# A hybrid diffusion backbone on one core: four weight-staging slots, another slot spacing, and a reordered opening

## The chip, the cores and the metric

The kernel runs on one core of a Trainium2 chip. The metric is the device time of one execution, in microseconds; the median of several executions of the same program is what is compared. The core has a matrix engine (PE, with weight loads shown apart as PEld), a vector engine (DVE), a scalar engine (ACT), a general engine (POOL) and a sync engine (SP) that only issues transfers. On-chip memory has 128 partitions; all addresses below are bytes inside one partition.

## What is computed

Two layers over 1024 latent tokens and 256 context tokens of width 1024, all in float32. The reference, cut to its frame:

```python
for i in range(DEPTH):                      # DEPTH = 2
    sh1, sc1, g1, sh2, sc2, g2 = ada_mod(c, ada_w[i], ada_b[i])
    u_lat = modulate(rms_norm(h_lat, norm1_g[i]), sh1, sc1)
    # the same for the context stream, with c_ctx
    if even:                                # layer 0
        y_lat = mixer_ab(u_lat, *ab)        # Fourier channels || Hyena long convolutions
        y_ctx = mixer_ab(u_ctx, *ab)
    else:                                   # layer 1
        y_lat, y_ctx = mixer_na(u_lat, u_ctx, ...)   # 2-D neighbourhood attention
    h_lat = h_lat + g1 * y_lat
    h_lat = h_lat + g2 * swiglu(modulate(rms_norm(h_lat, norm2_g[i]), sh2, sc2), gate, up, down)
return rms_norm(h_lat, final_g)
```

`ada_mod` is `silu(cond) @ w + b`. The Hyena filters come from a small sine network on positions (`sin(freq * (z @ w1 + b1))`, twice, then `@ w3`), are windowed, summed and Fourier-transformed before they are multiplied with the spectrum of the input.

## The kernel before

**Precision.** A float32 product is made of three faster ones. An operand x is split into a rounded part `hi` (ACT, L323) and the rest `lo` (DVE, L325); then hi·hi, hi·lo and lo·hi are added up in PSUM. In the profile these products are the MATMULs of 512, 384 or 256 columns at L319, L1503, L1674 and L1786. Every MATMUL has a weight load (LDWEIGHTS) of its own. A few products, those of the opening's adaLN and sine network among them, are plain float32 and take two passes of PE each.

**Stages, in order of time.** Opening (0 to about 190 us): sine network (`filter_mlp`), raw filters (`filter_raw`, DVE at L665), adaLN vectors of layer 0 (`ada_first`), norms of the input (`norms`), and the spectrum of the filters in two halves (`filter_spectrum`, 32 matrices `ff_l` of 512 KB, loaded by `cast`). Then input projection, Fourier and Hyena mixing (to about 700), output projection and the context part of FFN 0 (to about 1000), the Winograd-like FFN 0 (`wino_steps`, L1503, then `down`, L1674), the values and attention (about 1640 to 2260), and FFN 1 to the end at 2974.

**Memory.** Tiles are taken from pools; a pool gives each tag a ring of slots. From low addresses up: the descriptor area of the GpSimd-issued transfers (16 KB), constants (`cp`, with a pad of PAD_C words), `p4` (S4 tiles, 20 of 4 KB), `p2` (S2 tiles, 35 of 2 KB), `pg` (G), `pt` (T, six of 2 KB, with a pad of PAD_T words), `pk` (TK) and `pw`, the weight pool. `pw` has three tags with two slots each: `wl`, `wh` and `ws`. `weights` (L343) loads a matrix block into `ws` and splits it into `wh` and `wl`; `cast` (L389) loads a float32r matrix straight into one of the three tags in turn; `mat` takes `wh` and `wl` in turn; `cmat` and `cmat2` load f16 into `ws` and copy into `wh`/`wl`. `shifted` (L330) takes a tile of 1056 words and starts at word 16 of it, which sets the slot's size: 1056 words, 4224 bytes.

Added up from the pools of the built program, the first S4 slot starts at 20672 (80 x 256 + 192) and every S4, S2, G and T slot a multiple of 2048 behind it. The weight pool starts at 203968 (796 x 256 + 192), and its slots are 4224 (16 x 256 + 128) apart. So modulo 256 the moving operands start at 192, and the two slots of each weight tag at 192 and at 64.

**What sets the order.** The program is written as generators that `run` steps by hand (`next(ada1)`, `next(fr)`, `next(ng)`), and a scheduler of the tile layer then orders each engine's instructions within what the buffers and dependences allow. SP issues most loads (`ld`, L304), POOL those of `ldr` (L310), each in order; a transfer waits on its queue for the completion counter that it shares with the eighth one before it.

**The opening as written** (`run`, from L2057). `setup` loads `mask` and `gs`, `ada_begin` loads `ada_b`; then come the four loads of the sine network, `cond`, two blocks of `w3`, ten `x_row` blocks of 512 KB (`norms`, first step), then both layers of the sine network (`drain(mlp)`), eight adaLN steps, the eight steps of `filter_raw` with an adaLN step each, and the spectrum.

Of the kernel before, what the change touches and what calls it, by code (L numbers as in the profile page):

```python
# [10 lines left out]
F32 = mybir.dt.float32  # L11
F32R = mybir.dt.float32r
F16 = mybir.dt.float16
# [5 lines left out]
P = 128  # L19
# [9 lines left out]
WID = {0: 512, 1: 512, 2: 256, 3: 256, 4: 256}  # L29
OFF = {0: 0, 1: 512, 3: 512, 4: 768}  # L30
KSTART = (0, 8, 24, 32)
PAD_C, PAD_T, SHIFT = 72, 112, 16
BOPS = ("B11", "B21", "T2", "T1", "T3", "B22", "T4")


# [201 lines left out]
class Builder:  # L237
    def __init__(self, ctx, tc, a, out, taps=None, stop=None):
        self.tc, self.nc, self.a, self.out = tc, tc.nc, a, out
        self.taps, self.stop = taps, stop  # L240
        ent = ctx.enter_context
        self.cp = ent(tc.tile_pool(name="cp", bufs=1))
        self.p4 = ent(tc.tile_pool(name="p4", bufs=20))
        self.p2 = ent(tc.tile_pool(name="p2", bufs=35))
        self.pg = ent(tc.tile_pool(name="pg", bufs=4))
        self.pt = ent(tc.tile_pool(name="pt", bufs=6))
        self.pko = ent(tc.tile_pool(name="pk", bufs=4))
        self.pw = ent(tc.tile_pool(name="pw", bufs=2))
# [45 lines left out]
    def PQ(self):  # L294
        return self.pq.tile([P, 512], F32, tag="pq", name=self.nm("pq"))

    def C(self, w, dt=F32, p=P):
        return self.cp.tile([p, w], dt, name=self.nm("c"), tag=self.nm("ct"))

# [25 lines left out]
        self.last_lo = eng.tensor_tensor(lo, src, hi.bitcast(F32), SUB).ins  # L325

    def pair2(self, tags=("wh", "wl")):
        return [self.pw.tile([P, 1024], F32R, tag=g, name=self.nm(n)) for g, n in zip(tags, ("wh", "wl"))]

    def shifted(self, tag, name, w=1024):  # L330

        return self.pw.tile([P, 1056], F32R, tag=tag, name=self.nm(name))[:, SHIFT:SHIFT + w]

    def pair1(self):
        return self.shifted("wh", "wh"), self.shifted("wl", "wl")

    def pair3(self):

        self.p3 = (getattr(self, "p3", 0) + 1) % 3
        tags = ("ws", "ws") if self.p3 == 0 else ("wh", "wl")  # L340
        return [self.shifted(g, n) for g, n in zip(tags, ("wh", "wl"))]

    def weights(self, src, w=1024, cut=False, keep=None, wide=False, load=None):  # L343
        st = self.S4() if wide else self.pw.tile([P, 1024], F32, tag="ws", name=self.nm("ws"))
        if keep:
            hi, lo = keep
        else:
            hi, lo = self.pair3() if wide == 3 else self.pair1() if wide == 2 else self.pair2()
        (load or self.ld)(st.rearrange("p (n k) -> p n k", n=4) if cut else st[:, :w], src)
        self.split(st[:, :w], hi[:, :w], lo[:, :w])  # L350
        return hi, lo

    def mat(self, w, dt=F32R):
        self.mk ^= 1
        return self.pw.tile([P, w], dt, tag=("wh", "wl")[self.mk], name=self.nm("mat"))

    def cmat(self, w, src, view=None, small=False, shift=False):

        if small:
            st, m = self.S2(F16), self.S2(F32R, w)  # L360
            self.ld(view(st[:, :w]) if view else st[:, :w], src)
            self.nc.scalar.copy(m, st[:, :w])
            return m
        st = self.pw.tile([P, w], F16, tag="ws", name=self.nm("cs"))
# [6 lines left out]
        self.nc.scalar.copy(m, st)  # L371
        return m

    def cmat2(self, src, shift=False):

        st = self.pw.tile([P, 2048], F16, tag="ws", name=self.nm("cs"))
# [12 lines left out]
    def cast(self, w, src):  # L389

        self.mj = (self.mj + 1) % 3
        m = self.pw.tile([P, w], F32R, tag=("wh", "wl", "ws")[self.mj], name=self.nm("mat"))
        self.ldr(m, src)
        return m

# [33 lines left out]
    def setup(self):  # L429
        nc, a = self.nc, self.a  # L430
        self.ident = self.C(P)
        make_identity(nc, self.ident)
        self.ones = self.C(P)
        nc.vector.memset(self.ones, 1.0)
        self.eps = self.C(1)
        nc.vector.memset(self.eps, EPS)
        self.mask = self.C(4)
        self.ld(self.mask, a["mask"])
        self.gs = self.C(40)
        self.ld(self.gs, a["gs"])  # L440


    def ada_begin(self):
        nc, a = self.nc, self.a
        self.ada = {(l, c): self.C(48) for l in (0, 1) for c in (0, 1)}
        self.adab = self.C(96)
        self.ld(self.adab, a["ada_b"])

    def ada_first(self):
# [134 lines left out]
    def filter_mlp(self):  # L584
# [12 lines left out]
        for layer, w in enumerate((w1, w2)):  # L597
# [11 lines left out]
            self.clamp = nc.vector.tensor_scalar(s, s, 3.1415925, -3.1415925, op0=MIN, op1=MAX).ins  # L609
            self.sin = nc.scalar.activation(s, s, AF.Sin).ins  # L610
# [840 lines left out]
    def wino_weights(self, src, done=None, half=None):  # L1451


        nc = self.nc
        st = []
        if half is not None:
            for x in src:
                for c in (0, 512):
                    st.append(half())
                    self.ld(st[-1], x[:, c:c + 512])  # L1460
            a11, a12, a21, a22 = st
        else:
            for x in src:
                st.append(self.pw.tile([P, 1024], F32, tag="ws", name=self.nm("ws")))
                self.ld(st[-1], x)
            a11, a12, a21, a22 = (t[:, c:c + 512] for t in st for c in (0, 512))
        w = {} if done is None else done
        if done is None:
            wh = self.pw.tile([P, 1024], F32R, tag="wh", name=self.nm("wh"))
            wl = self.pw.tile([P, 1024], F32R, tag="wl", name=self.nm("wl"))  # L1470
# [182 lines left out]
    def down(self, l, bops, sops, hidc, hs, h, todo, after, keep):  # L1653
# [5 lines left out]
        def operands(asrc, bsrc, own):  # L1659
            hi, lo = self.S4(F32R), self.S4(F32R)  # L1660
            f = lo.bitcast(F32)
            if own:
                f = self.S4() if own == 1 else self.pw.tile([P, 1024], F32, tag="ws", name=self.nm("ws"))
# [98 lines left out]
        if l == 0:  # L1762
# [4 lines left out]
            for kb in range(NFB):  # L1767
# [289 lines left out]
    def run(self):  # L2057
        nc, a = self.nc, self.a
        self.setup()
        self.ada_begin()  # L2060
        raws = {sq: ({}, {}) for sq in ("l", "c")}

        def weave(main, *others):
# [5 lines left out]
        def drain(g):  # L2069
            for _ in g:  # L2070
                pass
# [3 lines left out]
        def norms():  # L2075
# [72 lines left out]
        weave(self.filter_spectrum("l", 1, raws["l"][1]), (ng, 1))  # L2148
        drain(ng)
        self.load_cond()  # L2150
# [305 lines left out]
```

## Time and profile before

| | |
|---|---|
| median of 3 executions | 2973.5 us (2970.81 to 2974.62) |
| the profiled execution | 2975.74 us |
| its span, first to last instruction | 2974.0 us |
| mean granted TensorE clock over the span | 0.982 |
| PE busy | 2843.4 us (96%) in 15704 matmuls |
| weight loads busy | 2357.7 us (79%) |
| DVE, ACT, POOL busy | 2095.6 (70%), 1327.3 (45%), 530.2 (18%) us |
| transfers | 567.36 MB, mean 191 GB/s |

A row of the profile names the source line, the engine, the operation and the tiles as `out<-in`, with buffer numbers left out: `ps<-s,wh` is a product into PSUM with moving operand `s` (an S4 or S2 tile) and weights `wh`. A matmul's own duration includes its way through the array, so in a dense run the distance from one start to the next is the pace, and it is much smaller than the duration. In a table by stretches, the columns are the stretch, its length, busy time and count for each engine, the granted clock (PEclk), the share of the DMA engines and GB/s. Line numbers are those of the kernel before; in the changed kernel they are 3 to 6 higher.

### The profile page before, as it was taken

How to read it: one execution, taken by the hardware profiler on the slowest of the kernel's cores; microseconds unless marked ns; L12 is line 12 of the kernel's file. 1: busy time of each engine (PE TensorE's matmuls, PEld its weight loads, DVE VectorE, ACT ScalarE, POOL GpSimd, SP SyncE). 2: the span in 40 equal slices, each digit the busy share in tenths (PEclk: the TensorE clock that was granted, in tenths of full speed). 3: DMA queues.
4: the chain of work that ended last, by engine and by line, in shares of the span. 5: the costliest groups of instructions: out<-in, count | busy, mean ns of one | idle time of the engine just before them, and what ended most of it. 6: DMA issues, size and time to landing. Idle time of an engine off the chain costs nothing. (4 is left out here: it accounts for less than half of the span.)

```text
span 2974.0 us, 44537 instructions
## 1 busy us (share of the span) xinstructions
PE 2843.4 (96%) x15704; PEld 2357.7 (79%) x15704; DVE 2095.6 (70%) x3984; ACT 1327.3 (45%) x2496; POOL 530.2 (18%) x816
## 2 busy tenths in 40 slices
PE   8999999699999999999999999999999999999997
PEld 3778888487899787788888888788787788888886
DVE  5877796775677777777777537888777977755455
ACT  4443215353454333333445326777765533333442
POOL 2112023251101111212010002232222022112000
PEclk9999999899999999999999999999999999999998
DMA  7765455274555554658885435777856266435653
GB/s 279 265 231 174 165 167 176 76 255 151 211 172 193 177 178 171 212 195 307 317 293 166 134 128 137 175 185 183 226 178 217 103 233 216 163 107 198 205 192 120
DMA packets 304813, 567.36 MB, mean 191 GB/s; under 512 B 83528, under 2 KB 130314, under 8 KB 304590
## 3 DMA queue, kind: packets, MB, share of 16 engines
q1 hardware_dynamic: 245950, 380.45, 40.3%
q0 software_dynamic: 56336, 179.87, 17.4%
q10 hardware_dynamic: 2304, 4.20, 0.4%
q8 instruction: 123, 2.02, 0.3%
q14 instruction: 100, 0.82, 0.1%
HBM read 414.44 MB, written 119.80 MB: 180 GB/s over the span
## 5 line engine op out<-in xcount | busy, mean ns | idle before, releaser
L1503 PE MATMUL ps<-s,s 128*128 128x512 f32 x1992 | 497.4, 390 | 6.9 <-ACT tk L1508 2.9
L1503 PEld LDWEIGHTS ps<-s,s 128*128 128x128 f32 x1992 | 373.2, 188 | 89.9 <-ACT g L1508 4.2
L319 PE MATMUL ps<-s,wh 128*128 128x256 f32 (+1 forms) x1768 | 394.3, 329 | 1.1 <-ACT wh L323 1.1
L319 PEld LDWEIGHTS ps<-s,wh 128*128 128x128 f32 x1768 | 294.5, 190 | 37.1 <-ACT wh L323 3.2
L319 PE MATMUL pq<-s,wh 128*128 128x512 f32 (+1 forms) x984 | 301.5, 384 | 4.1 <-DVE s L1900 3.7
L323 ACT CAST wh<-ws 128x1024 fp32r<-128x1024 f32 (+1 forms) x139 | 142.3, 1025 | 346.5 <-PE ps L319 179.0
L325 DVE TENSOR_TENSOR wl<-ws,wh 128x1024 fp32r<-128x1024 f32 (+1 forms) x139 | 165.6, 1193 | 140.0 <-ACT wh L323 139.6
L1674 PE MATMUL ps<-s,s 128*128 128x512 f32 (+1 forms) x1000 | 258.4, 383 | 3.9 <-DVE s L325 3.8
L319 PE MATMUL ps<-s,wl 128*128 128x256 f32 (+1 forms) x884 | 255.8, 327 | 1.5 <-DVE wl L325 1.5
L323 ACT CAST s<-s 128x1024 fp32r<-128x1024 f32 (+2 forms) x184 | 168.3, 940 | 188.4 <-DMA s<-d 167.3
L319 PE MATMUL ps<-s,s 128*128 128x64 f16 (+4 forms) x2659 | 218.0, 235 | 15.9 <-DVE st L1972 8.4
L323 ACT CAST s<-t 128x512 fp32r<-128x512 f32 (+1 forms) x241 | 136.8, 590 | 202.9 <-DVE t L1482 87.8
L325 DVE TENSOR_TENSOR s<-s,s 128x1024 fp32r<-128x1024 f32 (+2 forms) x162 | 185.1, 1174 | 47.7 <-ACT s L323 47.3
L1674 PEld LDWEIGHTS ps<-s,s 128*128 128x128 f32 x1000 | 184.4, 188 | 42.3 <-DVE s L325 5.9
L319 PE MATMUL ps<-s,mat 128*128 128x512 f32 x756 | 196.1, 411 | 19.9 <-ACT s L323 16.8
L319 PEld LDWEIGHTS pq<-s,wh 128*128 128x128 f32 x984 | 179.6, 191 | 39.1 <-DVE s L1900 5.3
L325 DVE TENSOR_TENSOR s<-t,s 128x512 fp32r<-128x512 f32 (+1 forms) x241 | 167.6, 710 | 45.5 <-ACT s L323 20.2
L1503 PE MATMUL ps<-s,wh 128*128 128x512 f32 x608 | 193.4, 395 | 0.2 <-DVE g L1596 0.2
L319 PEld LDWEIGHTS ps<-s,mat 128*128 128x128 f32 x756 | 146.6, 197 | 58.1 <-ACT s L323 14.6
L319 PE MATMUL pq<-s,wl 128*128 128x512 f32 (+1 forms) x492 | 183.4, 382 | 0.0
L319 PEld LDWEIGHTS ps<-s,wl 128*128 128x128 f32 x884 | 163.2, 189 | 18.8 <-DVE wl L325 2.3
L1674 PE MATMUL ps<-s 128*128 128x512 f32 (+1 forms) x500 | 149.4, 385 | 0.0
(431 smaller groups left out, 5499.2 us busy)
## 6 DMA issues: line engine op xcount, KB each, us to landing
s<-d SPq DMA_DIRECT2D x282, 256.0 KB, 3.7
s<-in_down SPq DMA_DIRECT2D x150, 256.0 KB, 4.1
d<-s POOLq DMA_DIRECT2D x137, 256.0 KB, 3.6
d<-tk POOLq DMA_DIRECT2D x98, 256.0 KB, 3.4
s<-in_ada_w POOLq DMA_DIRECT2D x48, 512.0 KB, 4.9
g<-in_bias SPq DMA_DIRECT2D x128, 192.0 KB, 3.0
ws<-in_up SPq DMA_DIRECT2D x44, 512.0 KB, 3.7
d<-g POOLq DMA_DIRECT2D x87, 256.0 KB, 3.2
```

The lines of the kernel that those rows point to most:

```text
L319: self.nc.tensor.matmul(o, l, r, start=st, stop=sp)
L323: self.last_hi = nc.scalar.copy(hi, src).ins
L325: self.last_lo = eng.tensor_tensor(lo, src, hi.bitcast(F32), SUB).ins
L1503: nc.tensor.matmul(ps, x[:, sl], y, start=first and j == 0 and x is wh and y is xh, stop=j == 3 and x is wl, skip_group_check=True)
L1674: m = nc.tensor.matmul(acc[j][:, c0:c1], x[:, sl], y[:, xs], start=first and k == 0, stop=last and k == 2, skip_group_check=True)
```

## The change

Seven edits that belong together:

1. The descriptor area goes from 16 KB to 4 KB (`dynamic_dma_scratch_size=4096`).
2. The `ws` tag gets four slots, and tiles are taken through a new helper `W`. The largest tile is 1088 words, so slots are 4352 bytes apart (17 x 256). With PAD_C at 24 and PAD_T at 88 the first S4 slot starts at 8192 (32 x 256) and the weight pool at 193536 (756 x 256): modulo 256 every S4, S2, G, T and weight slot starts at 0. A `shifted` tile starts at 64, before at 0 or 128.
3. `pair3`, `cast` and the context part of `down` use the additional `ws` slots.
4. T gets a seventh slot.
5. The loads of `mask`, `gs` and `ada_b` move behind those of the sine network and of `w3` (`setup_late`); `cond` and the first adaLN step come first.
6. Of the adaLN steps, four (in the built order: products 1 to 4 of 16) run on PE between the two layers of the sine network, the next four before the raw filters, and the rest among the raw filters and in the spectrum.
7. The ten `x_row` loads go behind the eight window loads of the raw filters, and their ten squares, one step each, into the spectrum.

```diff
-PAD_C, PAD_T, SHIFT = 72, 112, 16
+PAD_C, PAD_T, SLOT, SHIFT = 24, 88, 1088, 16
...
-        self.pt = ent(tc.tile_pool(name="pt", bufs=6))
+        self.pt = ent(tc.tile_pool(name="pt", bufs=7))
...
+    def W(self, tag, name, dt=F32, w=1024):
+        return self.pw.tile([P, w], dt, tag=tag, name=self.nm(name), bufs=4 if tag == "ws" else 2)
...
-        return self.pw.tile([P, 1056], F32R, tag=tag, name=self.nm(name))[:, SHIFT:SHIFT + w]
+        return self.W(tag, name, F32R, SLOT)[:, SHIFT:SHIFT + w]
...
-        self.p3 = (getattr(self, "p3", 0) + 1) % 3
-        tags = ("ws", "ws") if self.p3 == 0 else ("wh", "wl")
+        self.p3 = (getattr(self, "p3", 0) + 1) % 4
+        tags = ("ws", "ws") if self.p3 % 2 == 0 else ("wh", "wl")
...
-        self.mj = (self.mj + 1) % 3
-        m = self.pw.tile([P, w], F32R, tag=("wh", "wl", "ws")[self.mj], name=self.nm("mat"))
+        self.mj = (self.mj + 1) % 4
+        m = self.W(("wh", "ws", "wl", "ws")[self.mj], "mat", F32R, w)
...
+    def setup_late(self):
+        a = self.a
+        self.ld(self.mask, a["mask"])
+        self.ld(self.gs, a["gs"])
         self.ld(self.adab, a["ada_b"])
...
             x = s
+            if layer == 0:
+                yield
...
-                f = self.pw.tile([P, 1024], F32, tag="ws", name=self.nm("ws")) if kb % 3 < 2 else self.S4()
+                f = self.W("ws", "ws") if kb % 5 < 4 else self.S4()
...
-            with self.follow(self.last_hi):
-                for i, t in rows:
+            for i, t in rows:
+                with self.follow(self.last_hi):
                     nc.scalar.activation(t, t, AF.Square, accum_out=sq[:, i:i + 1])
+                yield
...
-        next(mlp)
         ada1 = self.ada_first()
         next(ada1)
+        next(mlp)
         next(fr)
-        next(ng)
+        self.setup_late()
+        next(mlp)
+        for _ in range(3):
+            next(ada1)
         drain(mlp)
-        for _ in range(8):
+        for _ in range(3):
             next(ada1)
         with self.tc.issue_after(self.clamp), self.tc.issue_after(self.sin):
             next(fr)
-        for i, _ in enumerate(fr):
-            next(ada1, None)
-            if i in (0, 4):
-                next(ng)
-        drain(ada1)
+        for _ in fr:
+            next(ada1)
+        next(ng)
         fr = self.filter_raw("l", raws["l"], (1,))
         for i, _ in enumerate(self.filter_spectrum("l", 0, raws["l"][0])):
-            if i >= 2:
+            next(ada1, None)
+            next(ng)
+            if i >= 6:
                 next(fr, None)
-            if i >= 11:
-                next(ng)
+        drain(ada1)
         weave(self.filter_spectrum("l", 1, raws["l"][1]), (ng, 1))
...
-    nc = _bacc.Bacc("TRN2", target_bir_lowering=False, num_devices=1)
+    nc = _bacc.Bacc("TRN2", target_bir_lowering=False, num_devices=1, dynamic_dma_scratch_size=4096)
```

The other lines of the diff replace `self.pw.tile(...)` by `self.W(...)` with the same shape and tag.

More of the change, by code (lines that the diff above doesn't have):

```diff
@@ L327, in pair2 @@
     def pair2(self, tags=("wh", "wl")):
-        return [self.pw.tile([P, 1024], F32R, tag=g, name=self.nm(n)) for g, n in zip(tags, ("wh", "wl"))]
+        return [self.W(g, n, F32R) for g, n in zip(tags, ("wh", "wl"))]
     def shifted(self, tag, name, w=1024):
-        return self.pw.tile([P, 1056], F32R, tag=tag, name=self.nm(name))[:, SHIFT:SHIFT + w]
+        return self.W(tag, name, F32R, SLOT)[:, SHIFT:SHIFT + w]
     def pair1(self):
@@ L337, in pair3 @@
     def pair3(self):
-        self.p3 = (getattr(self, "p3", 0) + 1) % 3
-        tags = ("ws", "ws") if self.p3 == 0 else ("wh", "wl")
+        self.p3 = (getattr(self, "p3", 0) + 1) % 4
+        tags = ("ws", "ws") if self.p3 % 2 == 0 else ("wh", "wl")
         return [self.shifted(g, n) for g, n in zip(tags, ("wh", "wl"))]
     def weights(self, src, w=1024, cut=False, keep=None, wide=False, load=None):
-        st = self.S4() if wide else self.pw.tile([P, 1024], F32, tag="ws", name=self.nm("ws"))
+        st = self.S4() if wide else self.W("ws", "ws")
         if keep:
@@ L354, in mat @@
         self.mk ^= 1
-        return self.pw.tile([P, w], dt, tag=("wh", "wl")[self.mk], name=self.nm("mat"))
+        return self.W(("wh", "wl")[self.mk], "mat", dt, w)
     def cmat(self, w, src, view=None, small=False, shift=False):
@@ L363, in cmat @@
             return m
-        st = self.pw.tile([P, w], F16, tag="ws", name=self.nm("cs"))
+        st = self.W("ws", "cs", F16, w)
         self.ld(view(st) if view else st, src)
@@ L374, in cmat2 @@
     def cmat2(self, src, shift=False):
-        st = self.pw.tile([P, 2048], F16, tag="ws", name=self.nm("cs"))
+        st = self.W("ws", "cs", F16, 2048)
         self.ld(st, src)
@@ L437, in setup @@
         self.mask = self.C(4)
-        self.ld(self.mask, a["mask"])
         self.gs = self.C(40)
-        self.ld(self.gs, a["gs"])
-    def ada_begin(self):
-        nc, a = self.nc, self.a
         self.ada = {(l, c): self.C(48) for l in (0, 1) for c in (0, 1)}
         self.adab = self.C(96)
+    def setup_late(self):
+        a = self.a
+        self.ld(self.mask, a["mask"])
+        self.ld(self.gs, a["gs"])
         self.ld(self.adab, a["ada_b"])
@@ L1463, in wino_weights @@
             for x in src:
-                st.append(self.pw.tile([P, 1024], F32, tag="ws", name=self.nm("ws")))
+                st.append(self.W("ws", "ws"))
                 self.ld(st[-1], x)
@@ L1468, in wino_weights @@
         if done is None:
-            wh = self.pw.tile([P, 1024], F32R, tag="wh", name=self.nm("wh"))
-            wl = self.pw.tile([P, 1024], F32R, tag="wl", name=self.nm("wl"))
+            wh = self.W("wh", "wh", F32R)
+            wl = self.W("wl", "wl", F32R)
             self.split(st[0], wh, wl)
@@ L1662, in operands @@
             if own:
-                f = self.S4() if own == 1 else self.pw.tile([P, 1024], F32, tag="ws", name=self.nm("ws"))
+                f = self.S4() if own == 1 else self.W("ws", "ws")
             self.ld(f[:, :512], asrc)
@@ L2059, in run @@
         self.setup()
-        self.ada_begin()
         raws = {sq: ({}, {}) for sq in ("l", "c")}
```

## The prediction, made before the changed kernel ran

> **What bounds the kernel now.** I read the busy shares first, then the table by stages, then PE's waits, and last the timeline of PE, because a bound engine must be read at the level of its single instructions. The busy shares and three stages of the table (columns: stretch, its length, PE, PEld, DVE, ACT, POOL busy with counts, granted clock, DMA share, GB/s):
>
> ```profile
> PE 2843.4 (96%) x15704; PEld 2357.7 (79%) x15704; DVE 2095.6 (70%) x3984; ACT 1327.3 (45%) x2496; POOL 530.2 (18%) x816
> ```
>
> ```profile
> 0.00:60.00 60.00, 45.31 (x114) 14.77 (x114) 24.93 (x46) 22.75 (x46) 12.85 (x30) 0.97 0.87 317
> 60.00:150.00 90.00, 86.02 (x368) 63.14 (x368) 74.79 (x123) 47.32 (x78) 12.39 (x23) 0.98 0.73 244
> ...
> 1760.00:2260.00 500.00, 473.57 (x4153) 407.11 (x4152) 382.35 (x966) 340.87 (x963) 130.52 (x185) 0.98 0.70 186
> ```
>
> PE is the bound: it lacks 131 us of the span (2974.0 - 2843.4), of which 14.7 lie in the first 60 us and 26.4 in attention (500 - 473.6). So there are two ways to gain: fill PE's holes, or make PE's own products shorter. The change tries the first in the opening and around the weight slots; the second follows from its addresses, and the following rows of PE (start, time, instruction, count) show why. They are two stretches of FFN 1:
>
> ```profile
> 2475.83 0.64 PE L1503 MATMUL ps<-s,wh 128*128 128x512 f32 x2
> ...
> 2481.43 2.43 PE L1503 MATMUL pq<-s,s 128*128 128x512 f32 x10
> 2483.70 2.88 PE L1503 MATMUL ps<-s,s 128*128 128x512 f32 x12
> 2486.42 0.62 PE L1503 MATMUL pq<-s,s 128*128 128x512 f32 x2
> ```
>
> ```profile
> 2420.99 0.62 PE L1503 MATMUL ps<-s,wh 128*128 128x512 f32 x2
> ...
> 2426.54 2.66 PE L1503 MATMUL ps<-s,s 128*128 128x512 f32 x11
> ```
>
> Between 2475.83 and 2481.43 lie eight turns of two `s,wh` products and one `s,wl` product, 24 in 5.60 us, or 233.3 ns from start to start. Between 2420.99 and 2426.54 are 24 again, in 5.55 us: 231.3 ns. The twelve `s,s` products of the same shape from 2483.70 to 2486.42 take 2.72 us: 226.7 ns. No stretch holds a wait. What differs is where the weights lie. An `s` weight starts at 192 modulo 256, as the moving operand does. A `wh`/`wl` pair always has one slot at 192 and one at 64, since slots are 4224 bytes apart. I read the 5.6 ns between 226.7 and the mean of the two (232.3) as the price of a start that differs by 128 modulo 256. It is paid by both members of a pair: a turn takes 0.70 us instead of 0.68, not one or two products of it.
>
> **Part 1: the slots' distance (edit 2).** After the change every S4, S2, G, T and weight slot starts at 0 modulo 256. The groups by form (count | busy, mean ns | idle) give the number of products:
>
> ```profile
> L1503 PE MATMUL ps<-s,s 128*128 128x512 f32 x1992 | 497.4, 390 | 6.9 <-ACT tk L1508 2.9 <-ACT g L1638 2.0 <-ACT g L1508 1.4
> ...
> L319 PE MATMUL pq<-s,wh 128*128 128x512 f32 x824 | 272.8, 403 | 4.1 <-DVE s L1900 3.7 <-DVE s L1887 0.3
> L1674 PE MATMUL ps<-s,s 128*128 128x512 f32 x936 | 247.8, 390 | 3.2 <-DVE s L325 3.2
> L319 PE MATMUL ps<-s,wh 128*128 128x512 f32 x712 | 238.4, 401 | 0.5 <-ACT wh L323 0.5
> L319 PE MATMUL ps<-s,mat 128*128 128x512 f32 x756 | 196.1, 411 | 19.9 <-ACT s L323 16.8 <-DVE s L325 1.8 <-DVE t L916 0.6
> L1503 PE MATMUL ps<-s,wh 128*128 128x512 f32 x608 | 193.4, 395 | 0.2 <-DVE g L1596 0.2
> L319 PE MATMUL pq<-s,wl 128*128 128x512 f32 x412 | 163.3, 401 | 0.0
> L1674 PE MATMUL ps<-s 128*128 128x512 f32 x468 | 142.2, 391 | 0.0
> L319 PE MATMUL ps<-s,wl 128*128 128x512 f32 x356 | 131.4, 398 | 0.0
> L1503 PE MATMUL ps<-s,wl 128*128 128x512 f32 x304 | 120.4, 397 | 0.0
> ```
>
> Even the means carry the sign: 390 ns with `s` weights, 395 to 403 with `wh` and `wl`. The `wh` and `wl` rows add up to 824 + 712 + 608 + 412 + 356 + 304 = 3216 products; 3216 x 5.6 ns = 18.0 us. The 756 products with `mat` weights have half of their slots at 192 already. Bounds for each are 0 and 5.6 ns; I take 2.3, below the middle, as their run is broken more often: 1.7 us. Of the 1236 `pq` products (824 + 412), I let half fall into stages where PE waits for DVE and ACT anyway (attention lacks 26.4 us of PE), so 618 x 5.6 = 3.5 us come to nothing. Part 1 gives 18.0 + 1.7 - 3.5 = **16.2 us**. The products of 256 columns with `shifted` weights stand at nothing: a shifted tile started at 0 or 128 against 192, a distance of 64 to either side, and starts at 64 against 0 now, which is 64 again. The ends of this part are 0 (the address is not the cause) and 19.7 (all of it on the path).
>
> A rule speaks against this part. The Trainium skill, "TensorE: Matmul & The Clock Gate", section "Step-by-step: what each phase is for", says that PE has two independent read ports, one for the streaming operand and one for the weights. By it the start of a weight tile would not matter to a running product, and the sum would lose these 16.2 us. The 233.3 against 226.7 ns above speak against it, but they do not exclude that another trait of `wh`/`wl` tiles is the cause; this is rival A.
>
> **Part 2: the opening (edits 5 to 7).** PE's timeline, with the idle time before a row and what ended it in brackets:
>
> ```profile
> 6.92 2.47 PE L319 MATMUL ps<-s,t 66*128 66x512 f32 x4 [6.92 <-DMA t<-in_w1f]
> 15.11 2.50 PE L319 MATMUL ps<-s,t 128*128 128x512 f32 x4 [5.72 <-ACT s L610]
> 17.55 8.95 PE L319 MATMUL ps<-mat,c 128*2 128x512 f32 x16
> ...
> 30.80 1.88 PE L319 MATMUL ps<-mat,c 128*2 128x512 f32 x4 [0.46 <-DMA mat<-in_ada_k]
> 33.01 1.88 PE L319 MATMUL ps<-mat,c 128*2 128x512 f32 x4 [0.34 <-DMA mat<-in_ada_k]
> ...
> 36.14 0.73 PE L319 MATMUL pq<-s,s 128*128 128x512 f32 x2 [1.25 <-DVE s L665]
> ...
> 66.00 8.46 PE L319 MATMUL ps<-s,mat 128*128 128x512 f32 x36
> ```
>
> The holes add up to 6.92 + 5.72 + 0.46 + 0.34 + 1.25 = 14.69 us, which is what the table lacks (60 - 45.31). The queue of SP, and what lands late:
>
> ```profile
> 0.73 0.40 SPq L304 DMA_DIRECT2D c<-in_mask  x1
> ...
> 1.66 0.42 SPq L304 DMA_DIRECT2D c<-in_ada_b  x1
> ...
> 2.60 0.29 SPq L304 DMA_DIRECT2D t<-in_w1f  x1
> ...
> 3.82 0.48 SPq L304 DMA_DIRECT2D c<-in_cond  x1
> ...
> 5.48 12.74 SPq L304 DMA_DIRECT2D s<-in_x_row  x10
> ...
> 21.74 11.37 SPq L304 DMA_DIRECT2D s<-in_win_l  x8
> ```
>
> ```profile
> 9.88 0.22 ACT L454 ACTIVATE c<-c 128x16 f32<-128x16 f32 x1 [7.87 <-DMA c<-in_cond]
> ```
>
> ```profile
> mat<-in_ada_k POOLq DMA_DIRECT2D x16, 512.0 KB, 6.4
> ```
>
> In the new order `cond` has the queue's first place (0.73), `zf` the second and `w1f` the third, which is that of `ada_b` (1.66). `w1f` took 6.92 - 2.60 = 4.32 us to release PE; so the first product starts at 1.66 + 4.32 = 5.98, and its hole shrinks by 0.9. `cond` took 9.88 - 3.82 = 6.06 and is there at 6.8; the first `ada_k` block, issued near 2 us as now, lands 6.4 later, at 8.4, just when layer 1 ends (5.98 + 2.47). Four adaLN steps take 8.95 us (16 rows at 17.55) and cover the sine's wait of 5.72 whole. But they are longer than it, and PE takes them in order: the second layer starts at 8.45 + 8.95 = 17.4 instead of 15.11, so all behind the sine network (the raw filters) is 2.3 us later, with four adaLN steps more done. The next four steps cover the second sine as the four at 17.55 do now. What is left is 5.98 and 0.7 for the small holes (their bounds: 0 and the 2.05 that 0.46 + 0.34 + 1.25 make): the opening gains 14.69 - 6.68 = **8.0 us**. Bounds: 0 (the filters' delay passes on) and 14.69 (no hole at all).
>
> The moved steps, each with its queue: the three small loads take 3 x 0.4 us of SP where nothing waits for them before the adaLN vector is finished. `win_l` passes the ten `x_row` loads, and with 12.74 us less ahead of it (34.80 was when DVE got to its first window, the row of 36.14 waits for that) its 1.25 us go. The `x_row` loads come as much later; their squares fill ACT in the spectrum (ACT is busy for 47.3 us of the 90 from 60 to 150), and the norms are needed only when the spectrum ends, near 190 us. As each spectrum step now starts with a square, about one block of the norms more is left at the end: 0 to 2 us, within the bounds above.
>
> **Part 3: two more slots in `ws`, a seventh T, the 4 KB area (edits 1, 3, 4).** PE's waits for the weight tiles (us, times, longest):
>
> ```profile
> PE pq L319 <- ACT mat L371: 3.6, 1, 3.6
> ...
> PE ps L1786 <- DVE wl L325: 2.9, 2, 2.1
> ...
> PE ps L319 <- DVE wl L325: 1.5, 3, 0.8
> ...
> PE ps L319 <- ACT wh L323: 1.1, 2, 0.6
> ...
> PE pq L1503 <- ACT wh L323: 0.9, 1, 0.9
> ```
>
> Together 10.0 us is the most that earlier loads can bring. These waits end on ACT and DVE splitting, which more slots bring forward only where the load was late, so I take a fifth: **2 us** (bounds 0 and 10; what is late next is the other operand, `s`, split by the same engines). The descriptor area costs nothing while POOL's transfers in flight fit into a quarter of it; the trace has no row for a full area. From below nothing; from above, rival E.
>
> **Sum.** 16.2 + 8.0 + 2 = 26.2 us. From the profiled execution, 2975.74, that makes 2949.5; the median shown, 2973.5, is 2.2 below that execution, so the forecast is 2947.3, rounded **2947**. About 5.9 us (0.2%) is what a measurement here can tell from no change.
>
> **Rivals.** *A, the pace is no matter of addresses.* `wh` and `wl` are written by ACT and DVE while PE reads; that could slow their reading as well. Against it: `s` weights are split by the same engines, and run at 226.7. Then 26.2 - 16.2 = 10 us are left: 2963.5. Chance 0.10.
>
> *B, the opening gives nothing*, because the 2.3 us of the second layer and the crowded transfers are passed on to the spectrum: 2947 + 8 = 2955. For it: the transfers of the first 60 us use 0.87 of the DMA engines. Chance 0.07.
>
> *C, slower: the common start is the wrong one.* In the trace the fast products have both operands at 192 modulo 256, and none has both at 0. If 0 is a slow start, the `s,s` products (1992 + 936 + 468 = 3396) go from 226.7 to 233.3 ns, +22.4 us; `wh`/`wl` from 232.3, +3.2; `mat`, 756 x (6.6 - 2.3), +3.3; less 10 for the opening and slots: +18.9, 2992. It decides from 10 us / 7368 products = 1.4 ns each. Nothing in the rows speaks for it but that they don't show the case. Chance 0.15 with E.
>
> *D, the mirror:* 0 is better than 192, and all `s,s` products gain what C would lose: 2947 - 22.4 = 2924.6. Chance 0.06.
>
> *E, the small area holds up POOL:* were only two `ff_l` loads under way at a time, one would land every 3.2 us (6.4 / 2, the row of `ada_k`), the 32 of the spectrum in 102 us instead of the 84 or so from 66 to 150: +18, and 2965; one at a time would cost 32 x 6.4 - 84 = 121 us. Within C's 0.15, at 0.03.
>
> **How the numbers follow.** The forecast has 0.62, A 0.10, B 0.07, D 0.06, C and E 0.15. The range 2918 to 2970 goes below D and takes in A, B and E's milder end; it leaves out C. Faster: forecast, B, D and most of A, 0.80; within 0.2% the rest of A, 0.05; slower C and E's harder end, 0.15.
>
> **What would show it.** Part 1: 24 `wh`/`wl` products of FFN 1 in 5.45 us in both slot pairs, with `s,s` still at 12 in 2.72; at 5.6 A holds, and `s,s` at 2.8 is C. Part 2: PE's first product near 6.0, no hole of more than 1 us from 8 to 17, the run of `s,mat` products of 66.00 near 58. Part 3: the five waits are gone or no longer. The forecast is wrong if PE's busy time does not fall by some 16 us.

## The result, and the profile after

The changed kernel takes **2957.9 us** (median of 6 executions, 2952.26 to 2962.1) against 2973.84 us for the kernel before (6 executions, 2965.17 to 2977.89). The ratio is 0.9948 with an interval of 0.993 to 0.9966. A second comparison of the same kernel, made with the experiments below, gave 0.9932 (0.9917 to 0.9948). So the gain is 16 to 20 us. The forecast was 2947, a gain of 26; the direction is right, the size is not, and the parts are off by more than their sum.

First the whole of PE, then three stretches of the opening (columns: stretch, its length, busy time of PE, PEld, DVE, ACT, POOL with counts, granted clock, DMA share, GB/s), all of the changed kernel, and the third stretch of the kernel before:

```profile
PE 2832.0 (96%) x15704; PEld 2359.7 (80%) x15704; DVE 2097.2 (71%) x3984; ACT 1328.6 (45%) x2496; POOL 528.5 (18%) x816
```

```profile
0.00:60.00 60.00, 50.89 (x147) 20.42 (x148) 37.71 (x65) 19.29 (x30) 14.92 (x34) 0.97 0.98 346
60.00:150.00 90.00, 80.70 (x313) 56.54 (x313) 59.02 (x99) 48.24 (x89) 10.21 (x20) 0.91 0.66 217
120.00:140.00 20.00, 12.81 (x42) 9.06 (x42) 20.00 (x33) 12.73 (x21) 1.06 (x2) 0.77 0.62 208
```

```profile
120.00:140.00 20.00, 17.01 (x71) 12.93 (x70) 18.63 (x34) 11.41 (x21) 2.65 (x5) 0.99 0.90 302
```

PE is busy for 11.4 us less than before (2843.4 - 2832.0), not for the 16 that the forecast asked for. In the first 60 us it does 5.6 us more (50.89 against 45.31), as was wanted. In the next 90 us it does 5.3 us less (80.70 against 86.02), at a clock of 0.91 instead of 0.98. The opening is filled, and the spectrum behind it is emptied by as much. The third row says where: from 120 to 140 us DVE is busy without a break (20.00 of 20, 18.63 before) while PE works for 12.8 us (17.0 before).

The timeline of PE shows both ends of it, the filled opening and the new hole:

```profile
4.87 2.47 PE L322 MATMUL ps<-s,t 66*128 66x512 f32 x4 [4.87 <-DMA t<-in_w1f]
7.27 9.11 PE L322 MATMUL ps<-mat,c 128*2 128x512 f32 x16
16.30 1.35 PE L322 MATMUL ps<-s,t 128*128 128x512 f32 x4
20.17 7.56 PE L322 MATMUL ps<-mat,c 128*2 128x512 f32 x16 [2.52 <-DMA mat<-in_ada_k]
...
53.34 1.66 PE L322 MATMUL ps<-s,mat 128*128 128x512 f32 x6
```

```profile
132.03 1.22 PE L322 MATMUL ps<-s,mat 128*128 128x512 f32 x2 [5.70 <-ACT s L326]
```

```profile
128.95 1.06 ACT L681 ACTIVATE s<-s 128x1024 f32<-128x1024 f32 x1 [1.71 <-DVE s L669]
...
130.42 1.05 ACT L682 ACTIVATE s<-s 128x1024 f32<-128x1024 f32 x1
131.38 0.60 ACT L326 CAST s<-tk 128x512 fp32r<-128x512 f32 x1
```

The first product is at 4.87 instead of 6.92, the wait for the sine (5.72) is gone, though 2.52 us of waiting for `ada_k` have come in behind the second layer, and products of the spectrum stand at 53 us. At 132 PE then waits 5.7 us for a split, and until 140 there are two more waits, of 0.80 and 0.69. The rows of ACT show what holds the split up: it comes behind two steps of the filters' sums (L681, L682), and the first of these, by the profile, waited for DVE's windowing of the second half's raw filters (L669). From 120 to 140 us DVE does six of these windowing products; the kernel before does two there (its L665).

**The tail.** In the changed kernel the last DMA that POOL issues starts 3.86 us before the end of the span, in the kernel before 10.35 us. Timeline of POOL, before and after (first line: the span):

```profile
core 0 of [0], span 2974.0 us
...
2963.65 0.71 POOL L310 DMA_DIRECT2D out_t<-g  x1 [0.85 <-DVE g L2348]
```

```profile
core 0 of [0], span 2957.4 us
...
2953.54 0.71 POOL L313 DMA_DIRECT2D out_t<-g  x1 [0.86 <-DVE g L2354]
```

No view of busy time shows what lies behind it, since waiting instructions aren't counted as busy. In the trace's list of instructions it is one DRAIN of POOL, at the end of the program: 9.55 us before, 3.08 us after. That is 6.5 us of the 16.6 by which the two spans differ (other executions of the changed kernel wander by 10 us, the DRAIN does not: 3.09 us in the second profile, whose span is 2944.1), and the forecast had it at nothing.

**The pace.** A run of FFN 1, timeline of PE after:

```profile
2464.92 0.62 PE L1507 MATMUL ps<-s,wh 128*128 128x512 f32 x2
...
2467.64 0.39 PE L1507 MATMUL pq<-s,s 128*128 128x512 f32 x1
2467.87 0.62 PE L1507 MATMUL ps<-s,wh 128*128 128x512 f32 x2
...
2470.59 2.43 PE L1507 MATMUL pq<-s,s 128*128 128x512 f32 x10
2472.86 5.60 PE L1507 MATMUL ps<-s,s 128*128 128x512 f32 x24
```

Twelve products with `wh` and `wl` take 2.72 us (2464.92 to 2467.64, and again 2467.87 to 2470.59): 226.7 ns each, the pace of the ten `s,s` products behind them (2.27 us). Here part 1 came out to the nanosecond. In attention it did not. The projection of the keys:

```profile
1935.25 0.73 PE L322 MATMUL pq<-s,wh 128*128 128x512 f32 x2 [0.84 <-DVE s L1904]
...
1936.05 0.62 PE L322 MATMUL pq<-s,wh 128*128 128x512 f32 x2
...
1936.74 0.62 PE L322 MATMUL pq<-s,wh 128*128 128x512 f32 x2
...
1937.44 0.62 PE L322 MATMUL pq<-s,wh 128*128 128x512 f32 x2
...
1938.12 0.62 PE L322 MATMUL pq<-s,wh 128*128 128x512 f32 x2
```

Each step from row to row is a turn of three products. After a wait the first turn takes 0.80 us, the next 0.69, 0.70 and 0.68; three at 226.7 would be 0.68. Runs in attention end after some 13 products, when others of 64 to 384 columns come in, so much of each is a slow start. The projection of the queries, a little later, never comes to the pace. Two rows of one unbroken run after the change, and two before:

```profile
1962.73 0.63 PE L322 MATMUL pq<-s,wh 128*128 128x512 f32 x2
...
1965.60 0.63 PE L322 MATMUL pq<-s,wh 128*128 128x512 f32 x2
```

```profile
1972.13 0.65 PE L319 MATMUL pq<-s,wh 128*128 128x512 f32 x2
...
1975.01 0.65 PE L319 MATMUL pq<-s,wh 128*128 128x512 f32 x2
```

Four turns lie between the two rows of each pair, twelve products in 2.87 and in 2.88 us, 239 and 240 ns each. In the code the queries read their moving operand through a rearranging view (`by_chunk`), and so does the output projection (`by_row`, 233 ns in unbroken runs); the keys do not. That the view is the cause is not shown, since no run changed it; that these 768 products gained next to nothing from the addresses is.

Over the whole trace of the changed kernel, from start to start, the first four products of 512 columns with `wh` or `wl` after a wait or a change of width take 233.2 ns in the mean, those beyond the fortieth 227.5; before the change it was 233.0 and 232.5. The groups say the same:

```profile
L322 PE MATMUL pq<-s,wh 128*128 128x512 f32 x824 | 271.0, 400 | 6.5 <-DVE s L1904 3.2 <-DVE s L2289 1.9 <-DVE s L1891 1.3
...
L1507 PE MATMUL ps<-s,wh 128*128 128x512 f32 x608 | 189.4, 390 | 0.0
```

The mean duration fell from 395 to 390 ns at L1507 (L1503 before), to that of `s,s`, and only from 403 to 400 at L322.

**FFN 0.** One stretch of the Winograd steps, before and after:

```profile
1000.00:1300.00 300.00, 292.48 (x1268) 238.25 (x1267) 227.52 (x448) 102.21 (x168) 53.65 (x99) 0.99 0.53 185
```

```profile
1000.00:1300.00 300.00, 300.00 (x1325) 248.51 (x1324) 236.32 (x465) 106.60 (x173) 55.81 (x103) 1.00 0.54 191
```

Before, PE lacked 7.5 us of 300 here; after, nothing. This is a gain that none of the waits counted in part 3 contained.

### The profile page after: what moved, and what is told of

Its sections match the earlier page's. It is cut to its first block, busy times and chain, and to the rows that moved or that the text cites. A ratio compares the mean times of both kernels' runs of the same rounds, so it can differ in the third digit from the quotient of the medians.

```text
span 2957.4 us, 44598 instructions
## 1 busy us (share of the span) xinstructions
PE 2832.0 (96%) x15704; PEld 2359.7 (80%) x15704; DVE 2097.2 (71%) x3984; ACT 1328.6 (45%) x2496; POOL 528.5 (18%) x816
## 3 DMA queue, kind: packets, MB, share of 16 engines
q10 hardware_dynamic: 2304, 4.20, 0.4%
## 5 line engine op out<-in xcount | busy, mean ns | idle before, releaser
L1507 PE MATMUL ps<-s,s 128*128 128x512 f32 x1992 | 494.5, 390 | 5.1 <-DVE s L1398 1.7
L1507 PEld LDWEIGHTS ps<-s,s 128*128 128x128 f32 x1992 | 374.0, 188 | 84.5 <-ACT g L1512 2.1
L322 PE MATMUL ps<-s,wh 128*128 128x256 f32 (+1 forms) x1768 | 394.5, 329 | 2.7 <-ACT wh L326 2.7
L322 PEld LDWEIGHTS ps<-s,wh 128*128 128x128 f32 x1768 | 295.0, 190 | 37.8 <-ACT wh L326 5.1
L322 PE MATMUL pq<-s,wh 128*128 128x512 f32 (+1 forms) x984 | 300.4, 382 | 6.7 <-DVE s L1904 3.2
L322 PE MATMUL ps<-s,wl 128*128 128x256 f32 (+1 forms) x884 | 256.7, 328 | 2.6 <-DVE wl L328 2.6
L322 PE MATMUL ps<-s,s 128*128 128x64 f16 (+3 forms) x2669 | 221.8, 236 | 18.6 <-DVE st L1976 8.5
L322 PE MATMUL ps<-s,mat 128*128 128x512 f32 x732 | 191.5, 411 | 25.8 <-ACT s L326 17.7
L322 PEld LDWEIGHTS pq<-s,wh 128*128 128x128 f32 x984 | 178.8, 190 | 39.8 <-DVE s L1904 5.0
L322 PEld LDWEIGHTS ps<-s,mat 128*128 128x128 f32 x732 | 142.0, 198 | 63.9 <-ACT s L326 20.2
L1507 PE MATMUL ps<-s,wh 128*128 128x512 f32 x608 | 189.4, 390 | 0.0
L322 PE MATMUL pq<-s,wl 128*128 128x512 f32 (+1 forms) x492 | 183.7, 380 | 0.0
L322 PEld LDWEIGHTS ps<-s,wl 128*128 128x128 f32 x884 | 164.2, 190 | 20.4 <-DVE wl L328 3.7
L313 POOL DMA_DIRECT2D d<-s x153 | 83.0, 544 | 391.9 <-DVE s L1356 116.5
```

The costliest lines, as they stand in the source:

```text
L313: self.last_ldr = self.nc.gpsimd.dma_start(out, in_).ins
L322: self.nc.tensor.matmul(o, l, r, start=st, stop=sp)
L1507: nc.tensor.matmul(ps, x[:, sl], y, start=first and j == 0 and x is wh and y is xh, stop=j == 3 and x is wl, skip_group_check=True)
```

## The experiments

Theory 1, formed from these rows: the area brings its tail of 6.5 us; the addresses bring 8 to 10 us, nearly all of it in dense runs; the opening brings nothing, because the second half's raw filters, begun at spectrum step 6 instead of 2, crowd DVE from 120 to 140 us. Its rival is the forecast's own split (addresses 16, opening 8, slots 2, area 0). Ratios are to the kernel before, measured side by side; 0.001 is 3 us. By the intervals, the difference of two ratios is good to 5 or 6 us to either side.

### The area alone, and half of it

```diff
-    nc = _bacc.Bacc("TRN2", target_bir_lowering=False, num_devices=1)
+    nc = _bacc.Bacc("TRN2", target_bir_lowering=False, num_devices=1, dynamic_dma_scratch_size=4096)
```

> The kernel before with one edit: the descriptor area 4 KB instead of 16 KB. Theory 1 (the area's size is paid at the end, where POOL empties its queue): the end of the program after PE's last product shrinks from 14.5 us to about 8 us, everything ahead of it keeps its pace, and the time falls by 6.5 us, to a ratio of 0.998. Theory 2 (the forecast's: the area costs nothing either way): no change, ratio 1.000, and the tail stays near 14.5 us. If the small area held up transfers, the spectrum from 60 to 190 us would be longer.

Measured: 2969.35 against 2977.39 us, ratio **0.9967** (0.9958 to 0.9977). The tail, timeline of POOL:

```profile
core 0 of [0], span 2971.1 us
...
2967.05 0.71 POOL L310 DMA_DIRECT2D out_t<-g  x1 [0.86 <-DVE g L2348]
```

The row shows 4.05 us from the last DMA to the end, 6.3 less than before; POOL's DRAIN is 3.26 us. (The profiled execution as a whole is only 2.9 us shorter than the one of before: single executions wander by some us over their length, so the tail is read from the trace and the time from the medians.) Theory 1 holds; the forecast's zero is wrong. The gain, 8.0 us by the medians and 9.8 by the ratio (lower end 6.8), is a little more than the tail; what the rest is stays open.

> The kernel before with an 8 KB area. Theory 1 (POOL's last wait grows in proportion to the area: 9.55 us at 16 KB, 3.08 to 3.3 at 4 KB, so 0.53 us per KB): POOL's last wait 5.2 us, the time 4.3 us below before (ratio 0.9985). Theory 2 (a threshold, below which the area is free): 3.1 us or 9.55 us, nothing between.

The same edit with 8192. Measured: 2969.23 against 2978.48 us, ratio 0.9968 (0.9953 to 0.9982).

```profile
core 0 of [0], span 2977.3 us
...
2972.32 0.71 POOL L310 DMA_DIRECT2D out_t<-g  x1 [0.85 <-DVE g L2348]
```

4.98 us to the end, the DRAIN 4.24 us, not the 5.2 of the straight line. The four sizes give 2.92 us at 2 KB (below), 3.0 to 3.3 at 4 KB, 4.24 at 8 KB and 9.55 at 16 KB. That would fit a cost of 0.5 to 0.6 us per KB (4.24 over 8, 9.55 over 16) beside some 3 us of another wait; no run took the two apart, and the expectation's proportion without a floor was wrong.

### The addresses alone

On the kernel before with the 4 KB area, two slots per tag and the old opening:

```diff
-PAD_C, PAD_T, SHIFT = 72, 112, 16
+PAD_C, PAD_T, SHIFT = 24, 112, 16
...
-        return self.pw.tile([P, 1056], F32R, tag=tag, name=self.nm(name))[:, SHIFT:SHIFT + w]
+        return self.pw.tile([P, 1088], F32R, tag=tag, name=self.nm(name))[:, SHIFT:SHIFT + w]
```

> The kernel before with a 4 KB area, slots 4352 bytes apart and every start at 0 modulo 256, but two slots per tag and the old opening. Theory 1 (the start decides the pace only in dense runs; elsewhere something else slows the products with wh and wl): beside the run with the 4 KB area alone it gains 7 to 9 us; in FFN 1 a run of 24 products takes 5.45 us, in attention only about 1 ns per product is won. Theory 2 (the forecast's): 16 us beside that run. Theory 3 (extra slots, not starts, made FFN 1 faster): no gain, and the runs of 24 stay at 5.55 to 5.60 us.

Measured: 2956.29 us, ratio **0.9933** (0.9918 to 0.9948), against 0.9967 for the area alone in the same comparison: 10 us for the addresses (13 by the medians). From the other side, the changed kernel with the addresses of before:

```diff
-PAD_C, PAD_T, SLOT, SHIFT = 24, 88, 1088, 16
+PAD_C, PAD_T, SLOT, SHIFT = 72, 88, 1056, 16
```

> The changed kernel with the addresses of before: slots 4224 bytes apart, starts at 192, weight slots at 192 and 64 modulo 256; four ws slots, the opening and the 4 KB area stay. Theory 1 (the addresses brought 8 to 10 us): 8 to 10 us slower than the changed kernel, runs of 24 products in FFN 1 back at 5.55 to 5.60 us. Theory 2 (the forecast's): 16 us slower. Theory 3 (more slots made the runs faster): no change.

> The changed kernel itself, beside the three others of this call. Every theory: a ratio to before between 0.993 and 0.996, POOL's last wait about 3.1 us. It is the base for the three.

Measured: 2967.82 us, ratio **0.997** (0.9955 to 0.9985), beside 2953.56 us and **0.9932** (0.9917 to 0.9948) for the changed kernel itself: 11 us (14 by the medians). Timeline of PE with the old addresses:

```profile
2484.41 0.64 PE L1507 MATMUL ps<-s,wh 128*128 128x512 f32 x2
...
2487.22 2.43 PE L1507 MATMUL pq<-s,s 128*128 128x512 f32 x10
```

Twelve products are back at 2.81 us (234 ns). The addresses are the cause: within each pair the number of slots and the area were the same, so the third theory falls. They bring 10 to 14 us, more than theory 1's ranges. Times alone would not quite shut out the forecast's 16; the count of products below does.

### Another distance

All `wh` and `wl` tiles at 64 modulo 256, moving operands at 0:

```diff
-        return [self.W(g, n, F32R) for g, n in zip(tags, ("wh", "wl"))]
+        return [self.shifted(g, n) for g, n in zip(tags, ("wh", "wl"))]
...
-            wh = self.W("wh", "wh", F32R)
-            wl = self.W("wl", "wl", F32R)
+            wh, wl = self.pair1()
```

> The changed kernel with all wh and wl tiles started at 64 modulo 256 (also the 512-column ones and the 256-column ones that were at 0), moving operands at 0. Theory 1 (256-column products run at 114 ns when the weights are 64 off and at 119 when they are not; 512-column ones want distance 0): 768 products of 256 columns gain 5 ns each, 4 us, and the 3360 of 512 columns lose up to 5 ns each, 0 to 17 us; net 4 us faster to 13 us slower. Theory 2 (a distance of 64 is free of the cost for both widths): 4 to 12 us faster than the changed kernel, with 227 ns in attention too.

Measured: 2964.31 us, ratio 0.9962 (0.9945 to 0.9978), 9 us slower than the changed kernel. Timeline of PE:

```profile
2472.78 0.63 PE L1506 MATMUL ps<-s,wh 128*128 128x512 f32 x2
...
2475.58 2.46 PE L1506 MATMUL pq<-s,s 128*128 128x512 f32 x10
2477.88 5.60 PE L1506 MATMUL ps<-s,s 128*128 128x512 f32 x24
```

Twelve in 2.80 us: 233.3 ns, as slow as a distance of 128. Theory 1 holds: products of 512 columns want the same start modulo 256, not just another distance than 128. In the changed kernel the `s,s` products, now with both starts at 0, keep 226.7 ns in the long runs of the FFNs (226.9 before, at 192), so 0 and 192 are equal as common starts, and rivals C and D are both out. The other half of the theory, that products of 256 columns run at 114 ns with weights 64 off, holds only in part: the 768 that this run moved went from 120.4 to 117.9 ns.

### The opening alone, and the rest without it

The kernel before with edits 5 to 7 and nothing else (its core below), and the changed kernel with the same lines taken back:

```diff
-        next(mlp)
         ada1 = self.ada_first()
         next(ada1)
+        next(mlp)
         next(fr)
-        next(ng)
+        self.setup_late()
+        next(mlp)
...
-            if i >= 2:
+            next(ada1, None)
+            next(ng)
+            if i >= 6:
                 next(fr, None)
```

> The kernel before with the new opening alone (order of loads, adaLN steps, x_row and squares); 16 KB area, old slots. Theory 1 (the lead is given back): PE's first product near 5 us and a lead of some 9 us at 40 us, gone by 150 us because the raw filters of the second half start four spectrum steps later and DVE then holds PE up; time unchanged or up to 3 us longer, ratio 1.000 to 1.001. Theory 2 (the forecast's): 8 us less, ratio 0.9973.

> The changed kernel with the opening of before, all else as changed. Theory 1: as fast as the changed kernel or up to 3 us faster (ratio to before 0.994 to 0.995). Theory 2 (the forecast's, the opening brings 8 us): 8 us slower than the changed kernel, ratio 0.9975.

Measured: 2978.81 us, ratio **1.0004** (0.9996 to 1.0012), and 2958.07 us, ratio **0.9927** (0.9911 to 0.9943). In the windows of the opening alone PE does 48.91 us in the first 60 (45.31 before), but 82.38 in the next 90 (86.02), and 12.90 from 120 to 140 (17.01). The second is level with the changed kernel itself (0.9948 and 0.9932). Both say that the new opening brings nothing: rival B's price and, by its place, the spectrum. To see whether the late raw filters are the mechanism, one number of the changed kernel goes back:

```diff
-            if i >= 6:
+            if i >= 2:
                 next(fr, None)
```

> The changed kernel with the raw filters of the second half begun at spectrum step 2 as before, not at step 6. Theory 1 (the late raw filters load DVE from 120 to 140 us, PE waits 6 us and the clock falls): the wait at 126 us is gone and the time is 5 to 9 us shorter than the changed kernel. Theory 2 (the second half's window loads come late because the ten x_row loads are ahead of them on SP, so that an earlier start helps nothing): no change, and PE or DVE waits for in_win_l instead.

Measured: 2943.64 us, ratio **0.9891** (0.9874 to 0.9907), 10 to 12 us faster than the changed kernel, more than theory 1's 5 to 9. Windows and the only waits of PE of over 1 us from 120 to 140:

```profile
60.00:150.00 90.00, 82.75 (x342) 59.71 (x340) 66.40 (x116) 51.73 (x95) 11.09 (x21) 0.94 0.73 235
120.00:140.00 20.00, 16.72 (x66) 13.01 (x65) 18.34 (x36) 9.61 (x19) 2.64 (x5) 0.91 0.82 259
```

```profile
131.42 1.08 PE L322 MATMUL ps<-s,mat 128*128 128x512 f32 x2 [2.55 <-ACT s L326]
```

The wait of 5.70 us is 2.55, DVE has air again (18.34 of 20) and does none of the second half's windowing there, and the clock from 120 to 140 is 0.91 instead of 0.77. The rival, that the second half's windows come too late to start earlier, falls. PE's thousandth product starts at 257.9 us, against 263.4 and 263.0 in the two profiles of the changed kernel, so about 5 of the 10 to 12 us lie in the opening; where the rest comes from was not followed.

> The changed kernel with the raw filters of the second half from spectrum step 0. Theory 1 (what counts is that DVE's work for the second half is spread over the first half): between 3 us faster and 2 us slower than with step 2, and 8 to 14 us faster than the changed kernel. Theory 2 (step 2 just happens to suit): as slow as the changed kernel.

With step 0: 2944.48 us, ratio 0.9882 (0.9864 to 0.9901), the same as with step 2. It isn't the one good number but the early start.

### The slots

The changed kernel with two `ws` slots and the tags in the order of before:

```diff
-        return self.pw.tile([P, w], dt, tag=tag, name=self.nm(name), bufs=4 if tag == "ws" else 2)
+        return self.pw.tile([P, w], dt, tag=tag, name=self.nm(name), bufs=2)
...
-        m = self.W(("wh", "ws", "wl", "ws")[self.mj], "mat", F32R, w)
+        m = self.W(("wh", "wl", "ws")[self.mj], "mat", F32R, w)
```

> The changed kernel with two ws slots (and the tags taken in the order of before), at the same starts and spacing, new opening, 4 KB area, seven T slots. Theory 1 (area and addresses carry the gain): within 3 us of the changed kernel, ratio 0.993 to 0.995. Theory 2 (the slots bring the 9 us by which FFN 0 catches up between 1100 and 1250 us): 9 us slower than the changed kernel, ratio 0.9965.

Measured: 2971.33 us, ratio 0.9976 (0.9965 to 0.9987), 13 us slower than the changed kernel beside its own runs of before (0.9932; 8 against the first comparison's 0.9948). Its stretch of FFN 0, and PE's wait there:

```profile
1000.00:1300.00 300.00, 286.99 (x1237) 235.16 (x1236) 223.38 (x435) 98.73 (x163) 53.52 (x99) 0.98 0.54 184
```

```profile
PE ps L1507 <- ACT g L1512: 13.0, 6, 5.2
```

Theory 2 of this run holds: with two slots PE lacks 13 us in this stretch, with four nothing. But the run with the addresses alone also has two `ws` slots, lacks 9 us there, and still ends level with the changed kernel (0.9933). It differs by the old opening and six T slots. So the worth of the slots is not a number of its own. What they give in FFN 0 is in part paid elsewhere: with four slots and the old opening PE is busy for 39.47 us in the first 60, against 45.31 before, and from 500 to 720 us it does 178.55 against 183.02. The starts of PE's products in those two runs, both with the old opening, say it more plainly: the thousandth comes at 267.8 us with four slots and at 259.8 with two, but from the 5000th to the 8000th it is 635.7 us instead of 645.7. (T has seven slots in the one and six in the other.) Which of T, opening and slots makes the 13 us with two slots was not tried apart.

### The best of them

Step 2 for the raw filters and a 2 KB area:

> The changed kernel with the raw filters of the second half at step 2 and a 2 KB area. Theory 1 (proportion): POOL's last wait about 2.0 us, ratio to before 0.9885 to 0.989, the best of all; the waits of POOL's transfers unchanged. Rival E of the prediction (a small area holds up transfers) at half the size: the spectrum stretches and the time is over 5 us longer than with 4 KB.

Measured: **2942.46** us against 2978.48, ratio **0.9874** (0.9857 to 0.9891).

```profile
core 0 of [0], span 2942.6 us
...
2938.88 0.71 POOL L313 DMA_DIRECT2D out_t<-g  x1 [0.84 <-DVE g L2354]
```

3.72 us to the end, against 3.86 with 4 KB, and a DRAIN of 2.92 us instead of the 2.0 of a proportion: almost nothing is left to gain at the tail. Nothing stretches either; rival E doesn't show at half its size. This version beats both kernels, the one before by 36 us and the changed one by 17 (0.9932 against 0.9874, each beside its own runs of before).

## Why the prediction came out as it did

The direction held, the measured time is inside the range, and 10 to 14 of the 16 to 20 us come from part 1, which the forecast had as the largest. But the sum is only roughly right: errors in three steps went against each other. That it came out as near as it did is in part luck: 6.5 us or more are the tail, which the forecast had at nothing.

- **Part 1, 16.2 us, measured 10 to 14.** The mechanism and its price per product were right in long runs (226.7 against 231 to 234 ns, and back, by moving addresses alone). The mis-sized term is "3216 x 5.6 ns". Both stretches that I read it from lie in FFN 1. There the products with `wh` and `wl` gained the whole price from start to start (232.4 to 226.9 ns). The 2304 of L322 gained 1.3 ns each (233.6 to 232.2), for two reasons: almost half of them are among the first four after a wait or a change of width, which take 232 to 234 ns with either set of addresses, and the 768 of the queries and the output projection don't come to the pace at all (239.0 to 238.7 and 233.7 to 233.1 ns). A row from attention, quoted beside the other two, would have shown that. Added up from the starts of the changed kernel and of the run with the old addresses, the products with `wh` or `wl` as weights bring 8.2 us, those with `mat` 2.5, 480 with `wh` or `wl` as the moving operand, which the count left out, 1.9, and those of 256 columns, put at nothing, lose 1.4: 11 in all.
- **The rule of two ports** (rival A). The Trainium skill, "TensorE: Matmul & The Clock Gate", section "Step-by-step: what each phase is for", gives PE two independent read ports. The runs speak against reading that as "the weights' address is free": with the same instructions, 226.7 ns became 233.3 when the weights moved by 64 bytes.
- **Part 2, 8.0 us, measured 0 (1.0004).** The working of the first 60 us held: first product at 4.87 (5.98 expected), sine covered, second layer late (16.30, against 15.11 before and 17.4 in the working), and 9.1 us of holes left in the first 60 where 6.7 were expected. The step that failed is that the sum stops at the first 60 us. I wrote that the squares fill ACT and that the rest lies "within the bounds above", and never listed DVE's work that the edit moves: the raw filters of the second half, from spectrum step 2 to step 6. They end up in a stretch where DVE was nearly full already (18.63 of 20 us from 120 to 140 before). Undoing that one number gave 10 to 12 us.
- **Part 3, slots 2 us.** The five waits that I added up, those for `wh`, `wl` and `mat`, did not shrink; they are 14.2 us after, against 10.0:

```profile
PE pq L322 <- ACT mat L374: 5.2, 4, 2.5
...
PE ps L1790 <- DVE wl L328: 2.8, 2, 1.4
PE ps L322 <- ACT wh L326: 2.7, 3, 1.6
PE ps L322 <- DVE wl L328: 2.6, 3, 1.4
...
PE pq L1507 <- ACT wh L326: 0.9, 1, 0.9
```

  What went was PE's idle time in FFN 0 (7.5 us in 300). In the profile before it stands as three waits of L1503 for `tk` and `g` (2.9, 2.6 and 2.0 us), which I left out since no weight tile is named in them. So "10.0 us is the most" was not a bound. By which way the slots remove them was not followed, and their worth in the whole kernel stays open, as said above.
- **Part 3, area: "from below nothing".** This is the plainest error, 6.5 of the gained us at the least. I bounded a loss and saw no reason for a gain; the profile before shows the 10.35 us behind POOL's last DMA, and the working never comes to the end of the span.
- **Rivals.** B's price of 8 us came true in the opening, but not for the reason that it gives: the second layer's delay and the transfers were the same with step 2 (16.65 us, DMA share 0.99), and there the gain came. C, D and E are refuted by runs: 0 as a common start costs nothing and gives nothing, and a 2 KB area holds nothing up.

## What to carry to other kernels

When a step is moved forward, follow the engines that it feeds to the end of the next stage, with the busy time of each in 20 us slices; a hole that is filled at 15 us can open again at 130. Read the price of an effect from every kind of place where it is to be multiplied, not from the cleanest run. And look at the last 20 us of the span before calling the size of a buffer or queue free.

## What the runs showed of the hardware

- A product of 512 columns in float32r goes at 226.7 ns in the long runs of the FFNs when weights and moving operand start alike modulo 256 bytes, at 231 to 234 ns when the slots of a pair lie at distances of 0 and 128, and at 233 at a distance of 64; common starts at 0 and at 192 are equal. For 256 columns no rule came out: with weights 64 off and moving operands at 0 in both, the context part of FFN 0 (800 to 1000 us) has a median of 113 ns in the changed kernel and of 118 in the run with the addresses alone.
- After a wait or a change of width, products of 512 columns start slowly even at equal starts and a granted clock of 1.0: with `wh` and `wl` the first four take 233.2 ns in the mean, and the `s,s` products of L322 234 in the same place, 228 from the fifth on.
- The queries' products of 512 columns stay at 239 ns in unbroken runs and the output projection's at 233, with either set of addresses.
- The DRAIN of POOL at the end of the program takes 9.55 us with a descriptor area of 16 KB, 4.24 with 8 KB, 3.0 to 3.3 with 4 KB and 2.92 with 2 KB.
- A hole of PE can cost more than its length. Behind the wait of 5.70 us the granted clock of the changed kernel is 0.50 from 131 to 141 us, and four products take 1.68 us (from 139.55) that take 0.90 from 142.16. How long a hole must be was not found: from 120 to 140 us, with longest waits of 1.73 us before and 1.78 in the run with the addresses alone, the clock is 0.99 and 0.83.
